# Moving weights read as two interleaved runs in a split-f32 decoder trunk

## The chip, the cores and the metric

The program runs on one core of a Trainium2 chip. The metric is the device time of one execution in microseconds. Engine names are those of the profile: PE multiplies matrices (PEld loads its stationary side), DVE and ACT do elementwise work, POOL is GpSimd, SP issues most DMAs.

## The reference, cut to what matters

Two layers over 256 tokens of width 1024. The first has full causal attention (one block of 256), the second a window of 128 with four shared key and value heads; each is followed by a gated feed-forward part with a causal convolution of width 3.

```python
for l in range(DEPTH):                       # DEPTH = 2
    if l < N_A:
        q, k, v = jnp.split(rmsnorm(x, attn_norm[l]) @ w_qkv_a[l], 3, axis=-1)
        ...                                  # rotary, causal attention of 16 heads
    else:
        k, v = jnp.split(rmsnorm(x, kv_norm) @ w_kv_b, 2, axis=-1)
        q = rmsnorm(x, attn_norm[l]) @ w_q_b[i]
        ...                                  # rotary, window of 128 with sinks
    x = x + o @ w_o
    x = x + conv_ffn(rmsnorm(x, ffn_norm[l]), w_up[l], conv_w[l], conv_b[l], w_down[l])
return rmsnorm(x, final_norm)
```

## The kernel before

All weights are f32. Each operand of a large product is split into a high part (type F32R, a rounded f32) and a low part (the rest, also F32R), and a product is the sum of three: high x high, high x low, low x high. Weights come in units of 128 x 2048 f32 (1 MB), which the host packs in the order of use: `fetch` loads a unit, ACT copies it to `wh` (line 157), DVE subtracts to give `wl` (line 160). `prepare(i + 4)` is called when unit i has been used, and four buffers rotate.

A matrix product on PE has a stationary side (128 x 128, loaded for each product) and a moving side, whose columns stream past it, up to 512 into one PSUM bank. Two kinds of product stand in the kernel:

- *Activations stationary, weights moving.* The projections (`proj`, lines 310 to 323: queries and keys, values, the shared keys and values with 512 columns, the second layer's queries with 256), the first values (`v_first`, line 739), and the products back to the residual, `Down` (lines 533, 534, 538: both attention outputs and both down products; 593 to 595: the last 512 columns in two pieces of 256). The weights' tiles are read column after column.
- *Weights stationary, activations moving.* The up product (lines 627 to 629), 256 tokens per product, so that the convolution along the tokens can run along a row.

Beside them there are transposes and small products of attention in full f32 (lines 264, 358, 463, 486).

The order of all work is set by the code itself: PE, ACT, DVE and SP keep the order in which the program is written, and a planner puts the small steps in between. It counts time by `tick`; for the three products of a projection chunk of n columns:

```python
            tick(3 * n / 2.4)
```

The program runs in stages: the first values and first group of queries and keys (to about 30 us), the first attention beside the remaining projections and the attention output (to about 120), the up product, the down product (about 225 to 284), the shared keys and values, second queries and second attention (to about 380), then up and down again (the last from about 490) and the closing norm.

Of the kernel before, what the change touches and what calls it, by code (L numbers as in the profile page):

```python
# [14 lines left out]
P = 128  # L15
D = 1024
S = 256
NB = S // P
KC = D // P
# [41 lines left out]
def trunk(ctx: ExitStack, tc, x, xw, pos, cpk, fin, sinks, w, out):  # L61
# [35 lines left out]
    def blk(b):  # L97
        return slice(b * P, (b + 1) * P)

    def half(n):  # L100
        return slice(n * 512, (n + 1) * 512)

# [11 lines left out]
    def tick(ns):  # L116
        clock[0] += ns
        while put_off and not busy[0]:
            item = min(put_off, key=lambda t: t[0])
            if item[0] > clock[0]:  # L120
                return
            run_item(item)
# [187 lines left out]
    def proj(o, hT, b, wv, units=()):  # L310

        n = o.shape[-1]
        for c in range(KC):
            require("x", b, c // 4)
            xh, xl = hx(hT, c)
            wh, wl = wv(c)
            nc.tensor.matmul(o, xh[:, blk(b)], wh, start=(c == 0), stop=False)  # L317
            nc.tensor.matmul(o, xh[:, blk(b)], wl, start=False, stop=False)  # L318
            nc.tensor.matmul(o, xl[:, blk(b)], wh, start=False, stop=(c == KC - 1))  # L319
            tick(3 * n / 2.4)  # L320
            if units and (c + 1) * len(units) % KC == 0:
                used(units[(c + 1) * len(units) // KC - 1])
            yield 3 * n / 2.4
# [190 lines left out]
    class Down:  # L514
# [6 lines left out]
        def mm(self, i, k, b, cols):  # L521
            if self.acc is None:
                self.acc = [[bank("acc") for _ in range(2)] for _ in range(NB)]
            need(self.u + i)
            self.wait(i)
            hi, lo = wq[self.u + i]
            ph, pl = self.parts[2 * i + k]
            first = i == 0 and k == 0
            end = k == 1 and (i == self.n_u - 1 or i == self.n_u - 2 and self.short and (b, cols[0][0]) == (1, 1))
            for n, c in cols:  # L530
                o = self.acc[b][n][:, c]
                s_ = slice(k * D + n * 512 + c.start, k * D + n * 512 + c.stop)
                nc.tensor.matmul(o, ph[:, blk(b)], hi[:, s_], start=first, stop=False)  # L533
                nc.tensor.matmul(o, ph[:, blk(b)], lo[:, s_], start=False, stop=False)  # L534
            for n, c in cols:
                o = self.acc[b][n][:, c]
                s_ = slice(k * D + n * 512 + c.start, k * D + n * 512 + c.stop)
                nc.tensor.matmul(o, pl[:, blk(b)], hi[:, s_], start=False, stop=end)  # L538
            tick(len(cols) * 3 * (c.stop - c.start) / 2.4)

        def units(self, lo, hi):
            for i in range(lo, hi):
                for k in range(2):
                    for b in range(NB):
                        self.mm(i, k, b, [(n, slice(0, 512)) for n in range(2)])
                        yield 6 * 512 / 2.4
                used(self.u + i)

        def finish(self, i0, after, tail=None, by_half=False):

            last = self.n_u - 1

            def unit(i, b, n):
                for k in range(2):
                    self.mm(i, k, b, [(n, slice(0, 512))])

            if by_half:
                for n in range(2):
                    for b in range(NB):
                        for i in range(i0, self.n_u):  # L560
                            unit(i, b, n)
                        self.add(b, n, after)
            for b in () if by_half else range(NB):
                for n in range(2):
                    for i in range(i0, last):
                        unit(i, b, n)
                    if b and n and tail is not None:
                        self.end(b, n, tail)
                    elif b:
                        unit(last, b, n)  # L570
                        self.add(b, n, after)
                if b == 0:
                    for n in range(2):
                        unit(last, b, n)
                        self.add(b, n, after)
            for i in range(i0, self.n_u):
                used(self.u + i)

        def end(self, b, n, tail):

            i = self.n_u - 1
            require("x", b, n)
            x_ = xr[b][:, half(n)]
            nc.vector.tensor_tensor(out=x_, in0=self.acc[b][n], in1=x_, op=ALU.add)
            need(self.u + i)
            self.wait(i)
            wh, wl = wq[self.u + i]
            for m in range(2):
                o = bank("u")[:, :S]
                for k in range(2):  # L590
                    ph, pl = (t[:, blk(b)] for t in self.parts[2 * i + k])
                    c = slice(k * D + n * 512 + m * S, k * D + n * 512 + (m + 1) * S)
                    nc.tensor.matmul(o, ph, wh[:, c], start=(k == 0), stop=False)
                    nc.tensor.matmul(o, ph, wl[:, c], start=False, stop=False)
                    nc.tensor.matmul(o, pl, wh[:, c], start=False, stop=(k == 1))
                tick(640)
                tail(m, o)

# [134 lines left out]
    def v_first(c):  # L733
        xh, xl = hx(hT, c)
        s_ = slice((c % 4) * 512, (c % 4 + 1) * 512)
        wh, wl = (t[:, s_] for t in wq[c // 4])
        for k, (a, m) in enumerate(((xh, wh), (xl, wh), (xh, wl))):
            for b in range(NB):
                nc.tensor.matmul(v_acc[b], a[:, blk(b)], m, start=(c == 0 and k == 0), stop=(c == KC - 1 and k == 2))  # L739
        tick(1280)  # L740

    def v_out(b, n, o):
# [298 lines left out]
def pack(inp):  # L1041

    import numpy as np

    def k_major(m):
        return m.reshape(m.shape[0] // P, P, m.shape[1])

    units = []
    m = k_major(inp["w_qkv_a"][0])
    q, k, v = (m[:, :, i * D:(i + 1) * D] for i in range(3))  # L1050
    qk = [np.concatenate([q[:, :, g * 256:(g + 1) * 256], k[:, :, g * 256:(g + 1) * 256]], axis=2) for g in range(4)]
    blocks = [v[:, :, :512], qk[0], qk[1], qk[2], v[:, :, 512:], qk[3]]

    def halves(blk):
        for a in range(2):
            units.append(blk[4 * a:4 * a + 4].transpose(1, 0, 2).reshape(P, UNIT))

    def rows2(mat):
        mm = k_major(mat)
        for i in range(mm.shape[0] // 2):  # L1060
            units.append(mm[2 * i:2 * i + 2].transpose(1, 0, 2).reshape(P, UNIT))

    def up(mat):
        mm = k_major(mat).reshape(KC, P, 2, NF, P)
        for i in range(NF):
            units.append(mm[:, :, :, i].transpose(1, 0, 2, 3).reshape(P, UNIT))

    for blk in blocks:
        halves(blk)
    rows2(inp["w_o_a"][0])  # L1070
    up(inp["w_up"][0])
    rows2(inp["w_down"][0])
    halves(k_major(inp["w_kv_b"]))

    order = [(2 * (j // 4) + e) * 4 + j % 4 for j in range(NH // 2) for e in range(2)]
    m = k_major(inp["w_q_b"][0].reshape(D, NH, HD)[:, order].reshape(D, D))
    for g in range(4):
        units.append(m[:, :, g * 256:(g + 1) * 256].transpose(1, 0, 2).reshape(P, UNIT))
    rows2(inp["w_o_b"][0].reshape(NH, HD, D)[order].reshape(D, D))
    up(inp["w_up"][1])  # L1080
    rows2(inp["w_down"][1])
    assert len(units) == N_UNITS
    wpk = np.stack(units)

    def feat(v_):
        return v_.reshape(-1, P).T

    cols = [feat(v_) for v_ in (inp["kv_norm"], inp["attn_norm"][1],
                                inp["ffn_norm"][0], inp["ffn_norm"][1])]
    for l in range(2):  # L1090
        four = np.concatenate([inp["conv_w"][l], inp["conv_b"][l][None]], axis=0)
        cols.append(four.reshape(4, 2 * NF, P).transpose(2, 1, 0).reshape(P, 2 * NF * 4))
    cpk = np.concatenate(cols, axis=1)
    return {
        "x": inp["x"].reshape(S, D),
        "xw": np.concatenate([feat(inp["attn_norm"][0])] + [
            t for c in range(KC) for t in (inp["x"].reshape(S, KC, P)[:, c].T, blocks[0][c])], axis=1),
        "pos": inp["positions"].reshape(NB, P).T,
        "cpk": cpk,
        "fin": inp["final_norm"],  # L1100
        "sinks": inp["sinks_b"].reshape(NH)[order],
        "w": wpk,
    }
# [19 lines left out]
```

## Time and profile before

| | |
|---|---|
| median of 3 runs | 568.06 us (568.05 to 568.49) |
| span of the profiled execution, first to last instruction | 565.9 us |
| what lies around that span, by the median | 2.2 us |
| PE busy | 558.0 us, 3858 products |
| DVE, ACT, POOL busy | 427.7, 379.6, 101.6 us |
| DMA | 100.99 MB, mean 178 GB/s |

No time of the profiled execution other than its span is listed; the runs' lowest and highest lie 2.1 and 2.6 us above it. A row of the table of groups names line, engine, operation, output and inputs, shape and count, then the busy time and the mean of one in ns. Products overlap in the records, so the duration of one (some 390 ns for 512 columns) isn't what it costs: that is the distance from its start to the next one's, which the timeline and the chain show.

### The profile page before, as it was taken

The numbers are of one execution on the slowest core, as the hardware profiler recorded it, in microseconds if no ns is written. First come the engines' busy times: TensorE is split into PE (matmuls) and PEld (weight loads), VectorE is DVE, ScalarE is ACT, GpSimd is POOL, SyncE is SP. The second block draws the span as 40 slices with busy tenths as digits, with TensorE's granted clock in tenths as the row PEclk, the third lists the DMA queues.
The fourth block names the chain that finished last, engine by engine and source line by source line (L and its number), as shares of the span: only waits on it lengthen the run. The fifth ranks groups of instructions, "written<-read, shape, count | busy, mean of one in ns | idle before, by whom it ended". The sixth has DMA issues, their size and how long they took to land.

```text
span 565.9 us, 10192 instructions
## 1 busy us (share of the span) xinstructions
PE 558.0 (99%) x3858; PEld 504.4 (89%) x3858; DVE 427.7 (76%) x928; ACT 379.6 (67%) x768; POOL 101.6 (18%) x124
## 2 busy tenths in 40 slices
PE   9999999999999999999999999999999999999995
PEld 7888888899999999988888988889999999988884
DVE  6798678589798888755369988788888888873414
ACT  6988777578577776743449798877657777664213
POOL 7321001012323222100001000002332333110003
PEclk9999999999999999999999999999999999999998
DMA  8974344442566566555542724142465555765201
GB/s 328 371 281 155 145 149 150 149 149 76 197 215 204 213 215 224 207 199 189 216 156 85 289 76 150 74 150 76 149 250 197 206 203 204 254 215 213 85 0 74
DMA packets 15311, 100.99 MB, mean 178 GB/s; under 512 B 1952, under 2 KB 2080, under 8 KB 3744
## 3 DMA queue, kind: packets, MB, share of 16 engines
q1 hardware_dynamic: 14976, 100.09, 49.4%
q8 instruction: 30, 0.49, 0.3%
q10 hardware_dynamic: 288, 0.26, 0.1%
q14 instruction: 17, 0.14, 0.1%
HBM read 99.30 MB, written 1.05 MB: 177 GB/s over the span
## 4 chain that ended last, share of the span: by engine, by line
PE 93%; ACT 3%; DVE 3%; issue 1%; POOL 0%; DVEq 0%; POOLq 0%; ACTq 0%
PE acc L533 9%; PE acc L534 9%; PE acc L538 9%; PE u L628 6%; PE u L627 6%; PE u L629 6%; PE t L628 6%; PE t L629 6%; PE t L627 6%; PE acc L317 4%; PE acc L319 4%; PE acc L318 4%; PE acc L739 2%; PE acc L627 2%; PE acc L628 2%; PE acc L629 2%
## 5 line engine op out<-in xcount | busy, mean ns | idle before, releaser
L160 DVE TENSOR_TENSOR wl<-wr,wh 128x1024 fp32r<-128x1024 f32 (+1 forms) x208 | 222.2, 1086 | 65.9 <-ACT wh L157 65.4
L157 ACT ACTIVATE wh<-wr 128x1024 fp32r<-128x1024 f32 (+1 forms) x208 | 189.8, 946 | 69.7 <-PE acc L538 55.5
L671 POOL TENSOR_TENSOR m<-m,m 128x256 f32<-128x256 f32 x44 | 64.7, 1470 | 176.3 <-DVE m L666 129.0
L533 PE MATMUL acc<-wh,q 128*128 128x512 f32 x238 | 94.5, 397 | 0.2 <-ACT q L492 0.2
L534 PE MATMUL acc<-wl,q 128*128 128x512 f32 x238 | 92.9, 391 | 0.0
L627 PE MATMUL u<-q,wh 128*128 128x256 f32 x320 | 88.4, 277 | 0.0
L628 PE MATMUL u<-q,wh 128*128 128x256 f32 x320 | 88.2, 276 | 0.0
L629 PE MATMUL u<-q,wl 128*128 128x256 f32 x320 | 88.0, 275 | 0.0
L629 PE MATMUL t<-q,wl 128*128 128x256 f32 x288 | 79.2, 275 | 0.0
L627 PE MATMUL t<-q,wh 128*128 128x256 f32 x288 | 79.2, 275 | 0.0
L628 PE MATMUL t<-q,wh 128*128 128x256 f32 x288 | 79.2, 275 | 0.0
L538 PE MATMUL acc<-wh,q 128*128 128x512 f32 x238 | 77.1, 389 | 0.0
L628 PEld LDWEIGHTS u<-q,wh 128*128 128x128 f32 x320 | 60.1, 188 | 0.0
L629 PEld LDWEIGHTS u<-q,wl 128*128 128x128 f32 x320 | 60.1, 188 | 0.0
L627 PEld LDWEIGHTS u<-q,wh 128*128 128x128 f32 x320 | 59.9, 188 | 0.0
L317 PE MATMUL acc<-wh,q 128*128 128x512 f32 (+1 forms) x160 | 57.1, 357 | 0.0
L319 PE MATMUL acc<-wh,q 128*128 128x512 f32 (+1 forms) x160 | 55.4, 346 | 0.0
L318 PE MATMUL acc<-wl,q 128*128 128x512 f32 (+1 forms) x160 | 55.2, 345 | 0.0
L627 PEld LDWEIGHTS t<-q,wh 128*128 128x128 f32 x288 | 54.1, 188 | 0.0
L628 PEld LDWEIGHTS t<-q,wh 128*128 128x128 f32 x288 | 54.1, 188 | 0.0
L629 PEld LDWEIGHTS t<-q,wl 128*128 128x128 f32 x288 | 54.1, 188 | 0.0
L533 PEld LDWEIGHTS acc<-wh,q 128*128 128x128 f32 x238 | 44.7, 188 | 9.7 <-ACT q L492 0.7
(167 smaller groups left out, 991.3 us busy)
## 6 DMA issues: line engine op xcount, KB each, us to landing
wr<-in_w SPq DMA_DIRECT2D x90, 1024.0 KB, 4.8
first<-in_xw SPq DMA_DIRECT2D x5, 384.0 KB, 5.6
xr<-in_x SPq DMA_DIRECT2D x2, 512.0 KB, 8.2
first<-in_xw SPq DMA_DIRECT2D x1, 768.0 KB, 7.0
fin_t<-in_fin SPq DMA_DIRECT2D x1, 512.0 KB, 6.0
out<-ot SPq DMA_DIRECT2D x1, 512.0 KB, 2.6
first<-in_xw SPq DMA_DIRECT2D x1, 388.0 KB, 3.5
out<-m ACTq DMA_DIRECT2D x1, 256.0 KB, 2.1
```

Of the source, the lines that this page charges most:

```text
L157: nc.scalar.activation(wq[i][0][:, c], raws[i][:, c], AF.Copy)
L160: nc.vector.tensor_tensor(out=wq[i][1][:, c], in0=raws[i][:, c], in1=f(wq[i][0][:, c]), op=ALU.subtract)
L317: nc.tensor.matmul(o, xh[:, blk(b)], wh, start=(c == 0), stop=False)
L318: nc.tensor.matmul(o, xh[:, blk(b)], wl, start=False, stop=False)
L319: nc.tensor.matmul(o, xl[:, blk(b)], wh, start=False, stop=(c == KC - 1))
L533: nc.tensor.matmul(o, ph[:, blk(b)], hi[:, s_], start=first, stop=False)
L534: nc.tensor.matmul(o, ph[:, blk(b)], lo[:, s_], start=False, stop=False)
L538: nc.tensor.matmul(o, pl[:, blk(b)], hi[:, s_], start=False, stop=end)
L627: nc.tensor.matmul(o, hi[:, s_], xh, start=(c == 0), stop=False)
L628: nc.tensor.matmul(o, hi[:, s_], xl, start=False, stop=False)
L629: nc.tensor.matmul(o, lo[:, s_], xh, start=False, stop=(c == KC - 1))
L671: nc.gpsimd.tensor_tensor(out=h, in0=gs, in1=t[1], op=ALU.mult)
```

## The change

On the host, the columns of every weight that moves are put in another order within each block of 512 (256 for the second layer's queries): all even columns, then all odd ones. On the chip, the moving side of each such product is a view that takes a column from the first run, then one from the second, 1 KB apart (512 B for blocks of 256), so that columns reach PE in their old order. The output is written as before, to neighbouring places, through a view in pairs. The stationary weights of the up product and the activations stay as they are.

```diff
+    def turns(t, n=None, at=0):
+        t = t.rearrange("p (a i) -> p i a", a=2)
+        return t if n is None else t[:, at // 2:(at + n) // 2]
+
+    def pairs(o):
+        return o.rearrange("p (i a) -> p i a", a=2)
...
     def proj(o, hT, b, wv, units=()):
         n = o.shape[-1]
+        o = pairs(o)
         for c in range(KC):
...
-            wh, wl = wv(c)
+            wh, wl = (turns(t) for t in wv(c))
...
-            for n, c in cols:
-                o = self.acc[b][n][:, c]
-                s_ = slice(k * D + n * 512 + c.start, k * D + n * 512 + c.stop)
-                nc.tensor.matmul(o, ph[:, blk(b)], hi[:, s_], start=first, stop=False)
-                nc.tensor.matmul(o, ph[:, blk(b)], lo[:, s_], start=False, stop=False)
...
+            part = [(pairs(self.acc[b][n]), slice(k * D + n * 512, k * D + (n + 1) * 512)) for n in cols]
+            for o, s_ in part:
+                nc.tensor.matmul(o, ph[:, blk(b)], turns(hi[:, s_]), start=first, stop=False)
+                nc.tensor.matmul(o, ph[:, blk(b)], turns(lo[:, s_]), start=False, stop=False)
+            for o, s_ in part:
+                nc.tensor.matmul(o, pl[:, blk(b)], turns(hi[:, s_]), start=False, stop=end)
...
-                    nc.tensor.matmul(o, ph, wh[:, c], start=(k == 0), stop=False)
...
+                    h_, l_ = (turns(t[:, c], S, m * S) for t in (wh, wl))
+                    nc.tensor.matmul(pairs(o), ph, h_, start=(k == 0), stop=False)
...
-                nc.tensor.matmul(v_acc[b], a[:, blk(b)], m, start=(c == 0 and k == 0), stop=(c == KC - 1 and k == 2))
+                nc.tensor.matmul(pairs(v_acc[b]), a[:, blk(b)], turns(m), start=(c == 0 and k == 0), stop=(c == KC - 1 and k == 2))
...
 def pack(inp):
+    def turns(m, n=512):
+        return m.reshape(*m.shape[:-1], -1, n // 2, 2).swapaxes(-1, -2).reshape(m.shape)
```

The host's `turns` is put around the blocks of `w_qkv_a`, `w_kv_b`, `w_q_b` (n = 256), and everything that `rows2` packs (both `w_o` and both `w_down`).

The instructions stand in the same order on every engine. On PE three products carry a wait that they did not have, and one transpose has one less. The first of the three follows transposes of the first attention's probabilities (`u` is their PSUM bank, `acc` that of a projection, `wh` and `wl` a weight unit, `q` the activations); before:

```order
L463 MATMUL u_614<-ident,m_36_508 128x128 [waits Activation_49]
L463 MATMUL u_614<-ident,m_36_508 128x128
L317 MATMUL acc_545<-wh_422,q_105 128x512
L318 MATMUL acc_545<-wl_423,q_105 128x512
L319 MATMUL acc_545<-wh_422,q_106 128x512
```

And after:

```order
L472 MATMUL u_614<-ident,m_36_508 128x128 [waits Activation_49]
L472 MATMUL u_614<-ident,m_36_508 128x128
L326 MATMUL acc_545<-wh_422,q_105 128x512 [waits PE_49]
L327 MATMUL acc_545<-wl_423,q_105 128x512
L328 MATMUL acc_545<-wh_422,q_106 128x512
```

Only the lines' numbers and the wait on PE's own count (PE_49) differ.

More of the change, by code (lines that the diff above doesn't have):

```diff
@@ L528, in mm @@
             first = i == 0 and k == 0
-            end = k == 1 and (i == self.n_u - 1 or i == self.n_u - 2 and self.short and (b, cols[0][0]) == (1, 1))
-            for n, c in cols:
-                o = self.acc[b][n][:, c]
-                s_ = slice(k * D + n * 512 + c.start, k * D + n * 512 + c.stop)
[L533 to L539, printed above, removed]
+            end = k == 1 and (i == self.n_u - 1 or i == self.n_u - 2 and self.short and (b, cols[0]) == (1, 1))
+            part = [(pairs(self.acc[b][n]), slice(k * D + n * 512, k * D + (n + 1) * 512)) for n in cols]
[4 more added lines that the diff above has]
+                nc.tensor.matmul(o, pl[:, blk(b)], turns(hi[:, s_]), start=False, stop=end)
+            tick(len(cols) * 3 * 512 / 2.4)
         def units(self, lo, hi):
@@ L544, in units @@
                     for b in range(NB):
-                        self.mm(i, k, b, [(n, slice(0, 512)) for n in range(2)])
+                        self.mm(i, k, b, range(2))
                         yield 6 * 512 / 2.4
@@ L554, in unit @@
                 for k in range(2):
-                    self.mm(i, k, b, [(n, slice(0, 512))])
+                    self.mm(i, k, b, [n])
             if by_half:
@@ L591, in end @@
                     ph, pl = (t[:, blk(b)] for t in self.parts[2 * i + k])
-                    c = slice(k * D + n * 512 + m * S, k * D + n * 512 + (m + 1) * S)
-                    nc.tensor.matmul(o, ph, wh[:, c], start=(k == 0), stop=False)
-                    nc.tensor.matmul(o, ph, wl[:, c], start=False, stop=False)
-                    nc.tensor.matmul(o, pl, wh[:, c], start=False, stop=(k == 1))
+                    c = slice(k * D + n * 512, k * D + (n + 1) * 512)
+                    h_, l_ = (turns(t[:, c], S, m * S) for t in (wh, wl))
+                    nc.tensor.matmul(pairs(o), ph, h_, start=(k == 0), stop=False)
+                    nc.tensor.matmul(pairs(o), ph, l_, start=False, stop=False)
+                    nc.tensor.matmul(pairs(o), pl, h_, start=False, stop=(k == 1))
                 tick(640)
@@ L1051, in pack @@
     qk = [np.concatenate([q[:, :, g * 256:(g + 1) * 256], k[:, :, g * 256:(g + 1) * 256]], axis=2) for g in range(4)]
-    blocks = [v[:, :, :512], qk[0], qk[1], qk[2], v[:, :, 512:], qk[3]]
+    blocks = [turns(t) for t in (v[:, :, :512], qk[0], qk[1], qk[2], v[:, :, 512:], qk[3])]
     def halves(blk):
@@ L1060, in rows2 @@
         for i in range(mm.shape[0] // 2):
-            units.append(mm[2 * i:2 * i + 2].transpose(1, 0, 2).reshape(P, UNIT))
+            units.append(turns(mm[2 * i:2 * i + 2]).transpose(1, 0, 2).reshape(P, UNIT))
     def up(mat):
@@ L1072, in pack @@
     rows2(inp["w_down"][0])
-    halves(k_major(inp["w_kv_b"]))
+    halves(turns(k_major(inp["w_kv_b"])))
     order = [(2 * (j // 4) + e) * 4 + j % 4 for j in range(NH // 2) for e in range(2)]
@@ L1077, in pack @@
     for g in range(4):
-        units.append(m[:, :, g * 256:(g + 1) * 256].transpose(1, 0, 2).reshape(P, UNIT))
+        units.append(turns(m[:, :, g * 256:(g + 1) * 256], 256).transpose(1, 0, 2).reshape(P, UNIT))
     rows2(inp["w_o_b"][0].reshape(NH, HD, D)[order].reshape(D, D))
```

## Prediction

> **What bounds the kernel now.** I read the page's busy shares first, then the chain of work that ended last, then PE's waits, and then how far apart products start.
>
> ```profile
> span 565.9 us, 10192 instructions
> PE 558.0 (99%) x3858; PEld 504.4 (89%) x3858; DVE 427.7 (76%) x928; ACT 379.6 (67%) x768; POOL 101.6 (18%) x124
> PE 93%; ACT 3%; DVE 3%; issue 1%; POOL 0%; DVEq 0%; POOLq 0%; ACTq 0%
> PE u L251 <- DVE warm L227: 1.1, 1, 1.1
> PE t L358 <- DVE m L352: 0.4, 1, 0.4
> PE acc L533 <- ACT q L492: 0.2, 1, 0.2
> ```
>
> A busy PE alone would prove little, since products overlap in the records. But 93% of the chain is PE, and PE's three listed waits add up to 1.7 us. The time is therefore the number of products times the distance between their starts. The three kinds of products, by line and shape, and what separates their starts (the chain for the down products, the timeline for the rest):
>
> ```profile
> L533 PE MATMUL acc<-wh,q 128*128 128x512 f32 x238 | 94.5, 397 | 0.2 <-ACT q L492 0.2
> L534 PE MATMUL acc<-wl,q 128*128 128x512 f32 x238 | 92.9, 391 | 0.0
> L538 PE MATMUL acc<-wh,q 128*128 128x512 f32 x238 | 77.1, 389 | 0.0
> L317 PE MATMUL acc<-wh,q 128*128 128x512 f32 x96 | 38.5, 401 | 0.0
> L317 PE MATMUL acc<-wh,q 128*128 128x256 f32 x64 | 18.6, 291 | 0.0
> L739 PE MATMUL acc<-wh,q 128*128 128x512 f32 x32 | 9.1, 405 | 0.0
> L739 PE MATMUL acc<-wl,q 128*128 128x512 f32 x16 | 4.9, 389 | 0.0
> L463 PE MATMUL u<-ident,m 128*128 128x128 f32 x96 | 13.8, 273 | 0.0
> ...
> 500.81 0.45 PE acc L538 x2
> 541.61 0.45 PE acc L538 x2
> ...
> 199.92 0.28 PE L627 MATMUL t<-q,wh 128*128 128x256 f32 x1
> 208.42 0.28 PE L627 MATMUL u<-q,wh 128*128 128x256 f32 x1
> ...
> 65.72 0.82 PE L463 MATMUL u<-ident,m 128*128 128x128 f32 x6
> ```
>
> In the down product the pair at L538 returns every six products. From 500.81 to 541.61 there are 30 rounds, 180 products: 40.80 / 180 = 226.7 ns for 512 columns. In the up product three lines take turns, and 25 rounds (75 products) lie between the two L627 rows: 8.50 / 75 = 113.3 ns for 256 columns. Both are 0.4427 ns per column, with no fixed part: 2 x 113.3 = 226.7. The six transposes of L463 are in full f32: their 0.82 us end one duration (0.273) after the last start, so five distances are 0.547 us, 109 ns per 128 columns, or 0.855 ns per column.
>
> A full-f32 column takes about twice a split one, but not quite: two columns of the fast kind need 0.885 ns where one of the slow kind needs 0.855, 3.5% less, although each transpose carries its fixed part inside. The kernel's own reckoning (line 320, tick) puts a column at 1/2.4 ns, 0.4167. Taking that as a cycle, 512 columns take 226.7 x 2.4 = 544 cycles, 17 for every 16 columns, and a transpose 262, of which 256 are two per column and some 2 ns are left over. So the fast kind loses one cycle in 17, in proportion to columns, and reads at half that speed lose next to nothing. It is this seventeenth cycle that is at stake.
>
> **The change, part by part.**
>
> *Reading.* Every product of 512 columns whose moving side is a weight now takes column i of one run and column i of another, 1 KB behind it, in turn. Those are 3 x 238 of L533 to L538, 3 x 96 of L317 to L319 and 48 of L739: 1050. Of 256 columns there are 3 x 64 at L317 to L319 (runs 512 B apart) and 12 in the tail: 204. The up products, whose moving side is the activation, stay as they are. No product of before reads its moving side in two runs, so the price is bounded from the nearest rows. Best case: a cycle per column and nothing else, 512 / 2.4 = 213.3 ns. With the transposes' leftover (109 - 106.7, about 2 ns) it is 215.5; if that leftover grows with columns, half a transposed column each, 0.427 ns, 218.9. Worst case: each column costs as much as a full-f32 one, 0.855 ns, 438 ns per 512. I take 215.5, near the best end: each run is then drained at half the speed, the speed at which the trace shows next to no loss. That reason is argued, not shown.
>
> The gain is 226.7 - 215.5 = 11.2 ns on 1050 products: 11.8 us. Not all of the 256s count. In the second attention the chain lies elsewhere:
>
> ```profile
> 310.00:350.00 40.00, 39.55 (x328) 36.62 (x327) 36.00 (x137) 33.95 (x96) 2.16 (x3) 1.00 0.46 162
> ...
> 326.50 0.95 ACT wh L157
> 331.36 1.22 DVE wl L160
> 339.63 1.13 DVE wl L160
> 346.81 1.23 DVE wl L160
> ```
>
> The columns of the first row are PE, PEld, DVE and ACT busy us, POOL, clock, DMA share and GB/s. DVE is busy 36.0 of 40 and ACT 33.95, and the chain of work runs through them, in the quoted rows from 326 to 348. Three of the four query groups run into it, 144 products. Their gain is covered by ACT and DVE, and I count it at nothing; only the first 48 and the tail's 12 count, about 5 ns each: 0.3 us.
>
> *Weight supply.* A unit of 2048 columns feeds 24 products of 512, 5.44 us now and 5.17 then. The layout is made on the host: the DMAs, the copies to wh and the differences to wl are the same instructions on the same addresses. They are the cover that must hold when PE runs faster:
>
> ```profile
> 225.00:284.00 59.00, 59.00 (x317) 50.99 (x316) 33.31 (x41) 27.75 (x36) 2.99 (x4) 1.00 0.55 200
> 30.00:115.00 85.00, 84.95 (x497) 69.75 (x496) 64.55 (x179) 64.14 (x148) 8.92 (x17) 1.00 0.46 163
> ACT wh L157 <- PE acc L538: 55.5, 20, 3.4
> ```
>
> In the first down product DVE is busy 33 of 59 us, ACT 28, the DMA engines 55%; ACT stood 55.5 us waiting for PE to release weight buffers. A demand 5% higher leaves all three below PE. If the cover went, a unit would be late by at most the 0.27 us gained on it. In the first attention (second row) DVE and ACT stand at 76% and its chains already make PE pause; I deduct a tenth of the gain of the 240 products there, 0.3 us.
>
> *Waits.* The instruction order is the same on all five engines. Three 512-column products now wait on PE's own count. The first of them follows transposes of the first attention's probabilities and stands ahead of the rest of PE's queue, so all of PE is behind it. Such a place before:
>
> ```profile
> 47.14 0.81 PE L463 MATMUL u<-ident,m 128*128 128x128 f32 x6
> 47.72 0.48 PE L317 MATMUL acc<-wh,q 128*128 128x512 f32 x1
> 48.03 0.39 PE L318 MATMUL acc<-wl,q 128*128 128x512 f32 x1
> ```
>
> There L317 already starts 0.31 us ahead of L318, 0.08 above the usual. A wait for the drain could cost from nothing (where it overlaps that pause) to 0.16 us (0.39 less 0.227); three make at most 0.5 us, and I take 0.2, near the covered end because one wait was removed too.
>
> *Writing.* The output is still 512 neighbouring f32 values, and a pair view of them is the same addresses; I cost it at nothing. If the pair view had a price it would be per column and is inside the bounds above.
>
> *Sum:* 11.8 + 0.3 - 0.3 - 0.2 = 11.6 us. The span goes from 565.9 to 554.3. The median of the runs shown, 568.06, is 2.2 us above the span; with the same 2.2 the time is 556.5. This case's own range runs from 552 (213.3 ns per 512 gives 14.1 us, all 204 of the 256s at 10 ns give 2.0, nothing deducted) to 562 (half of the excess stays, 7.0 us, less 0.7 for waits and pauses).
>
> [...]
>
> **The rivals.**
>
> *Each column opens its row of memory anew (slower, large).* Alternating between runs means that no two neighbouring reads lie together. If the reader holds only one piece at a time, a column costs as much as the slowest seen, 0.855 ns: 438 ns per 512, +211 ns on 1050 products, and 219 - 113 = +106 ns on 204: 222 + 22 = +244 us, about 812 us, since PE has no slack to hide it. It decides as soon as fetching a piece takes more than one column's time. The loss at full read speed speaks for it (the reader is at its limit already); that the loss is only 6% of full speed speaks against a reader with no spare. [...]
>
> *A mild loss: the excess doubles (slower).* If the lost cycle comes with each new stretch of memory and two runs bring twice as many starts per product, a 512 costs 240 ns: +13.3 on 1050 and +6.7 on 204, 15.3 us, 583 us. For it speaks that the distance isn't unique:
>
> ```profile
> 314.81 0.28 PE L317 MATMUL acc<-wh,q 128*128 128x256 f32 x1
> 316.00 0.28 PE L318 MATMUL acc<-wl,q 128*128 128x256 f32 x1
> ```
>
> Ten distances lie between these: 119 ns where 113.3 is usual, so a product can be pushed off its best rhythm. Against it: the 180 products of the down stage keep 226.7 throughout.
>
> *The order of reading is indifferent (no change).* If the seventeenth cycle belongs to each column's transport and not to where it lies, all 1050 stay at 226.7 and only the waits change: 568.1 to 568.6. For it speaks the exact proportion to columns in two shapes with different tiles; against it that transposes of the same operand width lose so little.
>
> **How the numbers follow.** The gain 0.54, no change 0.12, the mild loss 0.14, the large loss 0.20. Under 0.2% of the time, about 1.1 us, the measurement can't tell a change from none. Faster is thus 0.54, same 0.12, slower 0.34. The likeliest case's own range, 552 to 562, is widened over no change and the mild loss, which reaches from 583 to 590 if the excess comes out half as large again; that leaves out the 0.20 of the large loss. Predicted: 556.5, the likeliest case.
>
> **What would show it.** Right: in the down product the round of six shrinks from 1.36 to about 1.29 us, mean durations at L533 to L538 fall by some 11 ns, the up rounds stay at 0.34, and ACT's wait for PE falls from 55.5. Waits right: the first 512 after a transpose stays near 0.48. Wrong: a round of 1.44 (mild loss), or of 2.6 with PEld below half of PE (large loss); a round of 1.36 means that order is indifferent; a round of 1.29 with the time above 560 would mean that ACT, DVE or the DMAs had become the bound, seen in PE's waits on wh or wl.

## The result and the profile after

| | before | after |
|---|---|---|
| median | 568.05 us (568.01 to 568.49, 4 runs) | 559.22 us (558.66 to 559.50, 4 runs) |
| ratio to before | | 0.9841, 95% interval 0.9827 to 0.9855 |
| span of the profiled execution | 565.9 us | 557.4 us |

The change made the kernel 1.6% faster, 8.8 us. The forecast was 556.5, a gain of 11.6 us, so 2.7 us of it did not come. Of the page after, the busy shares and the chain (share of the span by engine):

```profile
span 557.4 us, 10191 instructions
PE 547.2 (98%) x3858; PEld 504.2 (90%) x3858; DVE 426.9 (77%) x928; ACT 379.0 (68%) x768; POOL 99.9 (18%) x124
PE 80%; DVE 8%; ACT 5%; DMA 4%; issue 1%; POOL 1%; DVEq 0%; POOLq 0%; ACTq 0%
L541 PE MATMUL acc<-wh,q 128*128 128x512 f32 x238 | 92.2, 387 | 0.2 <-ACT q L501 0.2
L542 PE MATMUL acc<-wl,q 128*128 128x512 f32 x238 | 90.6, 381 | 0.0
L544 PE MATMUL acc<-wh,q 128*128 128x512 f32 x238 | 74.6, 379 | 0.0
L635 PE MATMUL u<-q,wh 128*128 128x256 f32 x320 | 88.2, 276 | 0.0
```

PE's share of the chain fell from 93 to 80%; DVE, ACT and DMA took the rest. The lines of the change moved by some places (L533, 534, 538 are now L541, 542, 544), their mean duration fell by 10 ns, and the up product's stayed. How far apart products start in the last down product, from the chain:

```profile
500.08 0.43 PE acc L544 x2
501.38 0.43 PE acc L544 x2
540.23 0.43 PE acc L544 x2
```

From the first to the last row are 31 rounds of six: 40.15 / 186 = 215.9 ns, where it was 226.7.

1050 products at 10.9 ns are 11.4 us; 8.5 of them arrived in the span. PE's busy time fell by 10.8 us, so PE stood idle 2.3 us longer than before. Since the order of PE's instructions is unchanged, the start of the n-th product (counted from 0) can be set beside that of before. In us from the span's start:

| product | before | after | lead | products of 512 that read in turns since the row above, their worth |
|---|---|---|---|---|
| 240, in the first attention | 51.55 | 51.46 | 0.09 | 183, 2.0 |
| 660, in the first up product | 120.32 | 117.97 | 2.35 | 201, 2.2 |
| 1700, in the first down product | 239.15 | 236.70 | 2.45 | 8, 0.1 |
| 1980, shared keys and values | 301.49 | 296.46 | 5.03 | 266, 2.9 |
| 2580, in the second up product | 385.44 | 379.59 | 5.85 | 134, 1.5 |
| 3540, the same, later | 494.29 | 488.44 | 5.85 | none |
| last | 559.48 | 550.79 | 8.69 | 258, 2.8 |

The down products and the first attention beyond product 240 gave all or nearly all that they were worth, the up products nothing, the shared keys and values with the second attention half, the first 51 us almost nothing. The chain through the opening of the kernel after says why (start us, us, what):

```profile
17.38 8.93 DMA wr<-in_w
26.39 1.15 ACT wh L165 x2
...
30.14 1.22 DVE wl L168 x2
31.37 4.91 DMA wr<-in_w
36.38 2.01 ACT wh L165 x2
...
45.98 0.96 ACT wh L165
46.96 1.23 DVE wl L168
48.19 0.60 DVE q L373
...
51.33 0.63 PE t L367 x4
```

Weight loads, then their splitting by ACT and DVE, then a transpose on PE at 51.33. Before, PE reached its transpose at nearly the same moment, 51.41. The end of the PE rows ahead of it, after and then before (timeline):

```profile
50.65 0.38 PE L328 MATMUL acc<-wh,q 128*128 128x512 f32 x1
51.33 0.41 PE L367 MATMUL t<-ident,m 128*128 128x128 f32 x2 [0.30 <-DVE m L361]
```

```profile
50.98 0.39 PE L319 MATMUL acc<-wh,q 128*128 128x512 f32 x1
51.41 0.30 PE L358 MATMUL t<-ident,m 128*128 128x128 f32 x1
```

PE came 0.33 us earlier and waited 0.30 for DVE's rotated rows: what it had won it gave back there. It is one of five such waits. Before, PE waited for these rows once (0.4 us); after:

```profile
PE t L367 <- DVE m L361: 1.7, 5, 0.4
```

Three of the five lie in the first 52 us (1.06 us together), the other two at 308 and 331 us, in the second layer's queries and attention.

### The profile page after: what moved, and what is told of

Read it like the earlier page. It is cut to its first block, busy times and chain, and to the rows that moved or that the text cites. A ratio compares the mean times of both kernels' runs of the same rounds, so it can differ in the third digit from the quotient of the medians.

```text
span 557.4 us, 10191 instructions
## 1 busy us (share of the span) xinstructions
PE 547.2 (98%) x3858; PEld 504.2 (90%) x3858; DVE 426.9 (77%) x928; ACT 379.0 (68%) x768; POOL 99.9 (18%) x124
## 2 busy tenths in 40 slices
DMA packets 15311, 100.99 MB, mean 181 GB/s; under 512 B 1952, under 2 KB 2080, under 8 KB 3744
## 4 chain that ended last, share of the span: by engine, by line
PE 80%; DVE 8%; ACT 5%; DMA 4%; issue 1%; POOL 1%; DVEq 0%; POOLq 0%; ACTq 0%
PE acc L541 9%; PE acc L544 9%; PE acc L542 9%; PE u L634 7%; PE u L636 7%; PE u L635 7%; PE t L636 6%; PE t L634 6%; PE t L635 6%; DMA wr<-in_w 4%; DVE wl L168 3%; PE acc L634 2%; PE acc L636 2%; PE acc L635 2%; PE acc L326 2%; PE acc L328 2%
## 5 line engine op out<-in xcount | busy, mean ns | idle before, releaser
L541 PE MATMUL acc<-wh,q 128*128 128x512 f32 x238 | 92.2, 387 | 0.2 <-ACT q L501 0.2
L542 PE MATMUL acc<-wl,q 128*128 128x512 f32 x238 | 90.6, 381 | 0.0
L544 PE MATMUL acc<-wh,q 128*128 128x512 f32 x238 | 74.6, 379 | 0.0
L326 PE MATMUL acc<-wh,q 128*128 128x512 f32 (+1 forms) x160 | 55.9, 349 | 0.0
L328 PE MATMUL acc<-wh,q 128*128 128x512 f32 (+1 forms) x160 | 54.2, 339 | 0.0
L541 PEld LDWEIGHTS acc<-wh,q 128*128 128x128 f32 x238 | 45.0, 189 | 7.2 <-ACT q L501 0.8
```

Of the source, the lines that this page charges most:

```text
L541: nc.tensor.matmul(o, ph[:, blk(b)], turns(hi[:, s_]), start=first, stop=False)
L542: nc.tensor.matmul(o, ph[:, blk(b)], turns(lo[:, s_]), start=False, stop=False)
L544: nc.tensor.matmul(o, pl[:, blk(b)], turns(hi[:, s_]), start=False, stop=end)
```

## The experiments

Each starts from the changed kernel, and the kernel before stood at 568.0 to 568.2 us in the same sessions. `pairs_only` and the seven orders of reading were timed once each, the last four kernels four or five times. The diffs are shortened: the host's packing and the view of the outputs follow each.

**Is it the reading?** `pairs_only` keeps the pair view of the outputs and reads plain weights:

```diff
-        t = t.rearrange("p (a i) -> p i a", a=2)
+        t = t.rearrange("p (i a) -> p i a", a=2)      # natural order
 ...
-        return m.reshape(*m.shape[:-1], -1, n // 2, 2).swapaxes(-1, -2).reshape(m.shape)
+        return m
```

> Only the outputs go through the pair view; the weights lie and are read as before. If it is the reading in two runs that helps (theory A: one stretch of memory can't deliver a column per cycle without a lost cycle in seventeen, two stretches in turn can; or theory B: any pattern that isn't plain takes another path), products of 512 stay at 226.7 ns and the time at 568.1 +- 0.5. If the output's view makes the difference (theory C), 215.8 ns and 559.

568.3 us, 227 ns per 512: the output's view does nothing that shows. Theory C fell.

**Which orders of reading help?** Seven kernels pack the blocks of 512 in other ways, so that columns still come to PE in their natural order but lie elsewhere. In `runs4` and `step16` the number of runs is changed (4 and 128; `step8` has 256):

```diff
-        t = t.rearrange("p (a i) -> p i a", a=2)
+        t = t.rearrange("p (a i) -> p i a", a=4)      # 128 in step16, 256 in step8
```

> Four runs of 128 columns in turn (512 B apart) in every moving block of 512; blocks of 256 as in the change. Theories A and B: 215.8 ns per 512 and 559. If a reader holds only two stretches at a time (theory A, narrow): above 226.7 ns, up to the 438 ns of two cycles per column, 790 us.

> 128 runs of 4 columns: each column read lies 16 bytes behind the one before, so no two neighbouring reads share 16 bytes, and a stretch is met again only after 128 columns. Theory B: 215.8 ns and 559. Theory A, narrow (few stretches held), and the rule of the rival 'each column opens its row of memory anew': two cycles per column, about 430 ns per 512, some 780 us.

> 256 runs of two columns: each column read lies 8 bytes behind the one before, two on each 16 bytes, and a block of 512 is swept twice. Theory A: each 16-byte piece is fetched for two columns instead of four and the next is always another one; if a fetch is covered by two hits, 226.7 ns or a little less; if the fetch rate binds, 1.08 cycles per column of the step of 16 bytes (461 ns there, one hit) means about 230 ns per 512, 571 us. Theory B: 215.8 ns.

In `near16` and `near8` there are two runs again, but inside small blocks of 8 or 4 columns:

```diff
-        t = t.rearrange("p (a i) -> p i a", a=2)
+        t = t.rearrange("p (g a i) -> p g i a", g=64, a=2)   # g=128 in near8
```

> Two runs in turn, but only 16 bytes apart: blocks of 8 columns, even four in front of odd four. Theory B: 215.8 ns and 559, since the form of the pattern is kept. Theory A: the two runs lie in the same stretch, so the lost cycle stays: 226.7 ns and 568; between the two if a stretch is shorter than 32 bytes.

> Two runs in turn, 8 bytes apart: within every four columns the order in memory is 0, 2, 1, 3, so both runs lie in the same 16 bytes (tiles start on 16 bytes). The pattern has the same form as with 16 bytes. Theory A (one 16-byte piece can't deliver a column per cycle without the lost cycle, two in turn can): 226.7 ns per 512 and about 568. Theory B (the form of the pattern decides): 215.8 ns and 559.

In `two_each` and `four_each` the runs are 1 KB apart, and two or four columns are taken from each in turn:

```diff
-        t = t.rearrange("p (a i) -> p i a", a=2)
+        t = t.rearrange("p (a i j) -> p i a j", a=2, j=2)    # j=4 in four_each
```

> The two runs (1 KB apart) are read two columns each in turn: 8 bytes from one, 8 bytes from the other. If what helps is that two 16-byte pieces are met alternately (theory A), 215.8 ns per 512 and 559 stay. If each column has to come from another piece than the one before (A, strict), 226.7 ns and 568; something between says that the lost cycle is counted per pair of neighbours.

> The two runs are read four columns each in turn: each 16-byte piece is met once, whole, and only the next piece is a far one. Theory A (two pieces open at a time help): 226.7 ns and 568. If the lost cycle comes of going on to the neighbouring piece (theory D), 215.8 ns and 559.

The rate is read from the number of products that PE did in a stretch of the last down product, where there are only these. The rows are those of stretches of 40 us (60 for `step16` and `step8`); the columns are PE's busy us, the count, clock, DMA share and GB/s. In the order after, `near16`, `near8`, `four_each`, `runs4`, `two_each`, `step8`, `step16`:

```profile
500.00:540.00 40.00, 40.00 (x187) 1.00 0.36 130
```

```profile
500.00:540.00 40.00, 40.00 (x187) 1.00 0.35 130
```

```profile
505.00:545.00 40.00, 40.00 (x178) 1.00 0.37 132
```

```profile
525.00:565.00 40.00, 40.00 (x166) 1.00 0.27 99
```

```profile
550.00:590.00 40.00, 40.00 (x148) 1.00 0.23 79
```

```profile
600.00:640.00 40.00, 40.00 (x124) 1.00 0.16 53
```

```profile
720.00:780.00 60.00, 60.00 (x134) 1.00 0.05 18
```

```profile
720.00:780.00 60.00, 60.00 (x131) 1.00 0.08 31
```

A count takes in the products cut by the stretch's ends, some 1%. The distances below are means over the starts of the products of 512 in each trace that follow one of their kind without a pause (within 15% of the median); cycles are at the planner's 1/2.4 ns.

| kernel | ns per 512 | cycles per column | time us | 16-byte pieces as the even columns (and likewise the odd) meet them |
|---|---|---|---|---|
| before | 227.1 | 1.064 | 568.1 | two columns of each, pieces in sequence |
| near8 | 227.0 | 1.064 | 567.6 | two columns of each, in sequence |
| after | 215.8 | 1.012 | 559.2 | four columns of each, in sequence |
| near16 | 215.8 | 1.012 | 558.9 | four columns of each |
| four_each | 245.5 | 1.151 | 585.5 | two columns of each, then a far piece |
| runs4 | 274.0 | 1.284 | 614.5 | four columns of each, but two pieces by turns |
| two_each | 327.1 | 1.533 | 671.1 | two columns of each, and two pieces by turns |
| step8 | 454.9 | 2.132 | 803.7 | one column of each, in sequence |
| step16 | 462.6 | 2.168 | 811.1 | one column, every second piece |

Theory B, the form of the pattern, fell: `near8` has the form of `near16` and gains nothing. Theory D fell: `four_each` leaves the neighbouring piece each time and loses. Theory A as I had put it, two pieces open at a time, fell too: `two_each` and `four_each` touch the same two stretches in turn as the change does, and are slower than plain reading. What the fast orders (215.8 ns) share, and each of the others lacks in some part, is two runs and no more (in `runs4`, `step8` and `step16` each column comes from another run too, at 274.0 to 462.6 ns), one column from each in turn, and a distance between the runs for which 16 bytes are enough and 8 are not (215.8 and 227.0 ns).

The last column is a way of counting that I made after these runs. It takes the even and the odd columns apart and counts how many of each side fall in the same 16 bytes before that side moves on. Then plain reading has two on each side (columns 0 and 2, then 4 and 6), the change four, and all nine rates fall into order: one column to a piece goes with 2.13 and 2.17 cycles per column, two with 1.064, four with 1.012, and moving to and fro or far away with more (1.151 to 1.533). It fits nine measurements but no run tested it alone; a kernel that keeps two runs in turn and swaps their parity at every step would, and can't be written as one pattern of constant steps. So the alternation between two runs and the 16 bytes between them are shown; that the two sides are served apart is not.

The 811 us of `step16`, where each column lies in another 16 bytes than the one before, are the price that the prediction gave its rival, each column opening its row of memory anew (812). But sharing 16 bytes with the column before does not order the rates: in `step8` two columns in a row lie in the same 16 bytes, and a column still costs 2.13 cycles; in the change no column lies in the 16 bytes of the one before, and its products are, with those of `near16`, the fastest of the table (1.012). The order comes out if even and odd columns are counted apart, as in the table's last column.

**Is the opening's gain hidden?** `undo_opening` takes the change back in the first values and the first two groups of queries and keys:

```diff
-    blocks = [turns(t) for t in (v[:, :, :512], qk[0], qk[1], qk[2], v[:, :, 512:], qk[3])]
+    blocks = [v[:, :, :512], qk[0], qk[1]] + [turns(t) for t in (qk[2], v[:, :, 512:], qk[3])]
 ...
-            wh, wl = (turns(t) for t in wv(c))
+            wh, wl = wv(c) if plain else (turns(t) for t in wv(c))     # plain: g < 2
```

> The first values and the first two groups of queries and keys (144 products of 512, units 0 to 5) are packed and read as before; everything else as in the change. If the opening hides their gain (the chain there runs through weight loads, ACT and DVE), the time stays at the change's 559.2 +- 0.4. If it doesn't, 144 x 10.9 ns = 1.6 us come back: 560.8.

559.68 us (559.52 to 559.89), ratio 0.9854 (0.9840 to 0.9867): about 0.5 above the change's, not 1.6. Product 240 starts at 51.61 us in it, and at 51.45, 51.55 and 51.77 in `near8`, before and `pairs_only`, whose opening is as slow. In the five kernels whose opening has the fast rate (after, `near16`, `undo_queries`, `up_turned`, `up_hS`) it starts at 50.82 to 51.85, 51.20 in the mean. So some 0.4 of 1.6 us show in the opening, with a scatter of half a microsecond or more from run to run, and about 1.2 are hidden. PE's waits point the same way: of the 1.06 us for DVE's rotated rows in the first 52 us, 0.37 are left once the opening's products are slow again.

**And that of the second layer's queries?** `undo_queries` takes it back there (192 products of 256).

> The second layer's queries (192 products of 256) are packed and read as before, the rest as in the change. If their gain is hidden behind ACT and DVE but for the first group (48 x about 4 ns, 0.2 us): 559.2 to 559.8. If it isn't hidden, 192 x 5 ns, 1 us: 560.2.

559.21 us (558.73 to 559.61), ratio 0.9838 (0.9823 to 0.9853): no difference from the change's 559.22. In the trace the last product is at 550.70 against 550.79, though from product 1980 to product 2580 it takes 0.43 us more (83.56 against 83.13). Rather more than the 0.2 that I counted show there, and most of it is hidden or below what the times can tell.

**Can the up product have it too?** `up_turned` reads the activations of the up product in two runs; ACT and DVE write them in that order.

```diff
-                    xh, xl = hx(hT if i < n_raw else hS, c)
+                    xh, xl = (turns(t) for t in hx(hT if i < n_raw else hS, c))
 ...
+        # where hi and lo of hT and hS are written:
+        t.rearrange("p c (a i) -> p c i a", a=2)
```

> On top of the change the up product's moving activations are read in two runs as well (even tokens in front of odd ones, written that way by ACT and DVE): 2112 products of 256. If the gain is the lost cycle alone, they go from 113.3 to 109.2 ns (what 512 columns gave: columns / 2.4 + 2.5), 8.6 us, 550.6. If something with a period of 111.7 ns per product binds there, as in the second layer's queries after the change (111 to 112 ns), 3.4 us: 555.8. If the strided writes of ACT and DVE are slow, less, up to a loss.

557.52 us (556.94 to 558.16), ratio 0.9818 (0.9805 to 0.9832). In the up product 75 us hold eleven products more. First after, then `up_turned`, the same stretch:

```profile
140.00:215.00 75.00, 75.00 (x664) 1.00 0.60 212
```

```profile
140.00:215.00 75.00, 75.00 (x675) 1.00 0.60 212
```

The distance fell from 113.3 to 111.7 ns, not to 109.2: of the two numbers expected it is the second. The first carried over to 256 columns the 2.5 ns by which the 215.8 for 512 exceed 512 / 2.4; no run shows that for 256. What holds a product of 256 at 111.7 stays open (the weights of each are loaded on PEld beside it; no run took that away). But at each start of the up product 1 us was lost, so the time is 557.5 and not 555.8. The loss goes with writing to alternating runs, which took DVE 1.5 and ACT 1.8 times as long as plain writing (rows below). Two sets of activations are written so: hT, which the first four units read, and hS, for the rest. The chain of `up_turned` at that start runs through the two groups of DVE that write hT; in the change they take 415 and 284 ns:

```profile
L298 DVE TENSOR_TENSOR q<-y,q 128x256 fp32r<-128x256 f32 x16 | 9.8, 637 | 0.0
L297 DVE CAST q<-y 128x256 fp32r<-128x256 f32 x16 | 6.4, 422 | 0.0
```

The groups of DVE and ACT that write hS, `up_turned` first, then `up_hS`, which is the next kernel:

```profile
L660 DVE TENSOR_TENSOR q<-y,q 128x512 fp32r<-128x512 f32 x8 | 10.0, 1248 | 0.0
L659 ACT ACTIVATE q<-y 128x512 fp32r<-128x512 f32 x8 | 9.2, 1148 | 1.7 <-DVE y L657 1.5
```

```profile
L656 DVE TENSOR_TENSOR q<-y,q 128x512 fp32r<-128x512 f32 x8 | 6.5, 816 | 0.0
L655 ACT ACTIVATE q<-y 128x512 fp32r<-128x512 f32 x8 | 5.4, 671 | 1.9 <-DVE y L653 1.5
```

`up_hS` turns the order of the loop round: it writes each run of hS in sequence and reads the source at a step of two. The first four units of each up product, whose start is on the path, stay plain, and so does hT.

```diff
-        (700.0, lambda: nc.scalar.activation(hi, y_, AF.Copy)),
+        (700.0, lambda: nc.scalar.activation(two(hi), odd(y_), AF.Copy)),
 ...
+    def two(t): return t.rearrange("p c (a i) -> p c a i", a=2)
+    def odd(t): return t.rearrange("p c (i a) -> p c a i", a=2)
```

> On top of the change the up product's scaled activations (18 of 22 units in each layer, 1728 products of 256) are read in two runs; ACT and DVE write them in order and read the unscaled ones at a step of two instead, and the first four units stay plain. 1.7 ns a product as with up_turned, 2.9 us: 556.3, if the start of the up product costs nothing; 558 if the step of two costs ACT and DVE as much as the strided writes did (0.97 us at each start there).

556.20 us (555.42 to 556.94), ratio 0.9781 (0.9766 to 0.9796): faster than the kernel before and than the change, by 3.0 us, where 2.9 were expected. DVE's subtraction takes 816 ns as in the change (817), ACT's copy 671 instead of 628, and the start of the up product loses nothing: from product 600 to product 800 PE takes as long as after the change.

## Why the prediction was right, point by point

- *The bound.* Right: products times distance. Where PE is alone (the down products) the time fell as the distance did. At the faster rate it no longer holds in the opening and the second attention (see the cover).
- *The price of reading in two runs.* 215.5 ns was forecast, 215.8 measured, so 11.4 us instead of 11.8 for the 1050. The reason that I gave, that each run is drained at half speed, does not hold: `near8` drains each of its runs at half speed too and gains nothing, `two_each` does and takes 327 ns. So the size of this term was right by luck: 2 ns of leftover were carried over from the transposes, where nothing is read in two runs.
- *The 256s.* I counted 5 ns for 60 of them and nothing for 144. Those of the second layer's queries went from 113 to 120 ns down to 111 or 112, and undoing all 192 changes no time that can be told.
- *The cover.* This is the term that was mis-sized. I deducted 0.3 us for the first attention, from DVE's and ACT's 76% over the whole of it. Its opening is not like the rest: up to 51 us weight loads, ACT and DVE set the pace, and `undo_opening` shows about 1.2 us hidden there. The first attention behind it, for which I had made the deduction, gave its whole gain. Together with the shared keys and values and the second attention (0.8 us arrived of 1.5 for the 512s alone) the opening is where most of the missing 2.7 us went; what lies under half a microsecond is within the scatter of single profiles. In the down products the cover held: PE waited for no weights.
- *The waits.* Right, and the 0.2 us deducted do not show. The first 512 after transposes takes 0.46 us and starts 0.30 ahead of the next; before, these were 0.48 and 0.31:

```profile
46.98 0.82 PE L472 MATMUL u<-ident,m 128*128 128x128 f32 x6
47.55 0.46 PE L326 MATMUL acc<-wh,q 128*128 128x512 f32 x1
47.85 0.38 PE L327 MATMUL acc<-wl,q 128*128 128x512 f32 x1
```

- *The signs named.* The round of six went from 1.36 to 1.295 us, the up product stayed, and ACT's wait for PE's release of weight buffers fell from 55.5:

```profile
L165 ACT ACTIVATE wh<-wr 128x1024 fp32r<-128x1024 f32 (+1 forms) x208 | 189.5, 944 | 65.3 <-PE acc L544 50.8
```

- *The rivals.* No change and the mild loss did not come; the large loss is real, but for other orders (`step8`, `step16`). Between the change and these lie `four_each`, `runs4` and `two_each`. The second rhythm that I named (119 ns for 256) also stood in some 70 distances of the 512s before, at 228 to 236 ns; it is gone from the products that read in turns, where all 512s but those at pauses lie at 215 to 217.

## What to carry to other kernels

Where PE is the bound and its moving side is split f32, look at the distance between starts rather than at durations (226.7 ns against some 390 here). Most of the loss of 17 cycles for 16 columns went by the order of columns in memory (1.064 to 1.012 cycles per column), and the weights were packed for it on the host at no device time (DMA stayed at 100.99 MB, DVE went from 427.7 to 426.9 us busy, ACT from 379.6 to 379.0). Take one column from each of two runs, 16 bytes or 1 KB apart (215.8 ns both, 227.0 at 8 bytes), not two or four (327.1 and 245.5), and not from more runs (274.0 to 462.6): the neighbours of the good order that were tried here, other than the runs 8 bytes apart, made this kernel 3 to 43% slower than before. A gain per product was worth its full price only where PE was the last to arrive (2.8 us of 2.8 from product 3540 to the last, 0.1 of 2.0 before product 240); take the first microseconds (51 here), in which loads and splitting set the pace, out of the sum.

## What the runs showed of the hardware that I had not expected

- Two runs 16 bytes apart are as good as 1 KB (215.8 ns both), and 8 bytes apart are worth nothing (227.0).
- Two columns from each run in turn cost over two fifths more than plain reading (327 against 227 ns).
- Eight-byte steps cost almost what sixteen-byte steps do (455 and 463 ns), though two columns in a row lie in the same 16 bytes.
- Writing 128x512 f32 by ACT to two runs in turn took 1148 ns, reading them at a step of two and writing in order 671, plain 628; DVE's subtraction took 1248, 816 and 817.
